# Stated amounts of filler at the priority of the work around them, in a streaming-trunk layer on one core

## The chip, the core and the metric

The kernel runs on one core of a Trainium2 chip. TensorE (PE in the rows; PEld for its weight loads) multiplies into PSUM; VectorE (DVE), ScalarE (ACT) and GpSimd (POOL) work on tiles in SBUF; SyncE (SP) issues the DMAs. Each engine takes its instructions in the order of its own queue and waits at semaphores. The metric is device time in microseconds for one execution, the median of several runs.

## The reference, cut to what matters

One layer over 1024 prompt frames and 32 sample frames (together T = 1056), width 1024, in float32:

```
xn = rmsnorm(h);  u_a, u_b, v_b, q, k, v, gates = split(xn @ w_in)      # 256,256,256,512,512,512,3*1024
y_a = S5 state-space(u_a) -> gelu -> GLU          # branch A
y_b = u_b * (lower-triangular W_s per 128-chunk applied to layernorm(v_b))     # branch B, "sgu"
y_c = stick-breaking attention(q, k, v), 8 heads of 64                # branch C
h = h + (sum_i sigmoid(gates_i) * (y_i @ w_branch_i)) @ w_out
h = h + (silu(xn2 @ w_gate) * (xn2 @ w_up)) @ w_down, xn2 = rmsnorm(h);   y = rmsnorm(h)
```

It also returns k, v, the end states of the state-space branch and the normalised v_b of the sample rows.

## The kernel before, in words

Every float32 matrix product is three fast products, high by high, low by high and high by low part (`mm3`, lines 144 to 146). A weight unit is 128x1024 elements: a DMA into raw, a rounded copy wh by ACT (line 117), the remainder wl by POOL (line 118), in a ring of four. Tokens stand in two halves, 512 and 544 wide; `CHUNKS` cuts them into 512, 272 and 272 columns. So one unit of 128 output features over all tokens is 72 products (24 per chunk), and over the first half alone 24 products of 512 columns.

The first phase (to about 719 us of the trace) runs, in program order: norm and transposes of x; `s5_setup` (small DVE work on the state-space parameters, with a few transposes and products); `v_dense` (values); the query and key tasks of head pairs 0 and 1; `sgu`; `ua_dense` and `s5_main` (state space); `attention`. Beside them stands a list of filler tasks: `qk_dense` for each of four head pairs (k and q, 72 products each) and `gate_ahead`, the gate products with sigmoid for 7 blocks of the first half and 4 of the second, three branches each; their results go to DRAM (sig_d, line 949) and are fetched in the second phase. `fill(us)` takes steps of filler off the list until their estimated PE time adds up to us; `finish` takes all of one task. In `sgu` there is no fill.

A list scheduler then makes each engine's queue: of the instructions that it holds for ready it takes the one with the lowest priority number, which counts up in program order. From the sgu stage on, `fill` adds `low[0]` = 4000 (`LATER`) to that number around its steps (lines 957 to 961), so filler comes after everything within the next 4000 that is ready. What is left of the list is done behind the attention, before the second phase (gates and branches, output projection, feed-forward), which this change leaves alone.

PSUM has tags of two buffers each: t (transposes), z (scores and state space), d (all dense products of the first phase), av (attention output, key transposes, the GLU).

Attention runs 32 units (head pair, block of 256 rows tp, head h2; the last pair with tp reversed). `stage_a`: two loads of q (line 768), score products into z (lines 781 to 785), a sigmoid on ACT (787), a reversed running product on DVE (789). `stage_b`: transposes of the weights (811), a split by ACT and DVE (819, 820), products with the values into av (828, 829). `load_head` (lines 736 to 752) brings a head's keys kst and its value differences vt; the single load at line 747 is one row. It is called when the first `stage_a` of the head runs, which is one unit ahead of its `stage_b`. The sample rows' attention stands after unit 30.

In `s5_main`, U is loaded from DRAM (line 624), V = products of U (631), a DVE chain of ten large operations makes the state (641 to 653), the end state is transposed (660), the output products follow (677 to 679), a gelu, a round trip through DRAM, a split on DVE (699) and the GLU.

## Time and profile before

| | us |
|---|---|
| runs shown | 1815.08, 1830.27, 1834.05; median 1830.27 |
| the profiled execution | 1818.52 |
| its span, first to last instruction | 1816.8 |
| PE busy | 1702.1 (94%) |
| DVE, ACT, POOL busy | 692.2, 521.7, 534.7 |
| mean granted TensorE clock | 0.973 |

Busy times are of all instructions of an engine; a busy PE isn't PE at its peak, since matmuls overlap. The granted clock is a share of 2.4 GHz. In a group row, "idle before" is idle time of the engine just before these instructions, with what ended it.

### The profile page before, as it was taken

The page shows a single profiled execution, that of the slowest core. Times are in us where ns is not written, and L with a number is a line of the kernel's source. Part 1 is how long each engine was busy: PE and PEld are TensorE (multiplying, and loading weights), DVE is VectorE, ACT ScalarE, POOL GpSimd, SP SyncE. Part 2 cuts the span into 40 slices and gives each one's busy share as a digit, 9 for nine tenths or more (in the row PEclk, how much of TensorE's full clock was granted, in tenths as well). Part 3 has the DMA queues.
Part 4 walks back from the last instruction along what each step waited for, and adds up shares of the span by engine and source line. Part 5 has one row for each costly group of instructions (what it writes and reads, how often), then busy time and mean ns, then how long its engine had stood idle before and what let it go on. Part 6 is the DMA issues. An engine that isn't in the chain of part 4 may idle for free.

```text
span 1816.8 us, 25700 instructions
## 1 busy us (share of the span) xinstructions
PE 1702.1 (94%) x10421; PEld 1502.1 (83%) x10421; DVE 692.2 (38%) x1387; ACT 521.7 (29%) x914; POOL 534.7 (29%) x333
## 2 busy tenths in 40 slices
PE   6889898978878999999999899999999999999997
PEld 6888787756656798889998899889889888888886
DVE  7954516228888100550266601230230321321315
ACT  5222232326656232222223322112111111111124
POOL 3211212320002242534443233233323333333334
PEclk9999999989999899999999999999999999999999
DMA  6544252555455453773362211111111111111102
GB/s 192 133 101 104 86 131 77 160 175 136 131 129 147 165 158 91 223 255 96 91 193 67 82 47 47 41 32 56 38 45 47 47 47 47 47 47 47 47 24 96
DMA packets 246487, 178.18 MB, mean 98 GB/s; under 512 B 60060, under 2 KB 222912, under 8 KB 246368
## 3 DMA queue, kind: packets, MB, share of 16 engines
q1 hardware_dynamic: 246368, 176.53, 33.4%
q8 instruction: 82, 1.34, 0.3%
q14 instruction: 37, 0.30, 0.1%
HBM read 136.69 MB, written 39.21 MB: 97 GB/s over the span
## 4 chain that ended last, share of the span: by engine, by line
PE 62%; DVE 7%; DMA 3%; SPq 3%; issue 2%; ACT 1%; POOL 1%; POOLq 0%; DVEq 0%; ACTq 0%
PE p L146 18%; PE p L145 18%; PE p L144 18%; DMA vt<-v_d 2%; PE p_d L146 2%; PE p_d L144 2%; PE p_d L145 2%; DVE om L789 2%; SPq L747 1%; PE p L1179 1%; DVE rs_m L169 1%; DVE wtl L820 1%; POOL wl L118 1%; DMA raw<-in_w_in_dram 0%; DVE xb L181 0%
## 5 line engine op out<-in xcount | busy, mean ns | idle before, releaser
L118 POOL TENSOR_TENSOR wl<-raw,wh 128x1024 fp32r<-128x1024 f32 x164 | 402.1, 2458 | 889.8 <-ACT wh L117 836.7
L145 PE MATMUL p<-x,wh 128*128 128x272 f32 (+1 forms) x1056 | 342.5, 324 | 0.0
L144 PE MATMUL p<-x,wh 128*128 128x272 f32 (+1 forms) x1056 | 341.5, 323 | 0.0
L146 PE MATMUL p<-x,wl 128*128 128x272 f32 (+1 forms) x1056 | 341.5, 323 | 0.0
L117 ACT ACTIVATE wh<-raw 128x1024 fp32r<-128x1024 f32 x164 | 172.7, 1059 | 482.0 <-PE p L146 185.0
L144 PE MATMUL p_d<-xnh,wh 128*128 128x272 f32 (+1 forms) x648 | 222.1, 343 | 9.0 <-DVE QS L313 4.4
L146 PE MATMUL p_d<-xnh,wl 128*128 128x272 f32 (+1 forms) x648 | 220.2, 340 | 1.3 <-POOL wl L118 1.3
L145 PE MATMUL p_d<-xnl,wh 128*128 128x272 f32 (+1 forms) x648 | 219.8, 339 | 0.0
L144 PEld LDWEIGHTS p<-x,wh 128*128 128x128 f32 x1056 | 198.9, 188 | 16.0
L145 PEld LDWEIGHTS p<-x,wh 128*128 128x128 f32 x1056 | 198.8, 188 | 15.9
L1135 DVE TENSOR_TENSOR sl<-p,sl 128x272 f32<-128x272 f32 (+1 forms) x66 | 34.6, 525 | 463.8 <-PE p L146 463.8
L146 PEld LDWEIGHTS p<-x,wl 128*128 128x128 f32 x1056 | 198.7, 188 | 15.3
L144 PEld LDWEIGHTS p_d<-xnh,wh 128*128 128x128 f32 x648 | 125.9, 194 | 21.0 <-DVE QS L313 4.8
L1138 POOL TENSOR_TENSOR act<-sl,act 128x512 fp32r<-128x512 f32 (+2 forms) x66 | 61.1, 925 | 279.0 <-ACT act L1136 279.0
L1189 DVE TENSOR_TENSOR h<-p,h 128x512 f32<-128x512 f32 x160 | 108.1, 687 | 79.3 <-PE p L146 79.3
L145 PE MATMUL p<-wl,act 128*128 128x512 f32 x352 | 137.1, 390 | 1.2 <-POOL wl L118 1.2
L146 PE MATMUL p<-wh,act 128*128 128x512 f32 x352 | 137.1, 389 | 0.0
L144 PE MATMUL p<-wh,act 128*128 128x512 f32 x352 | 136.9, 389 | 0.0
L146 PEld LDWEIGHTS p_d<-xnh,wl 128*128 128x128 f32 x648 | 125.4, 194 | 12.0 <-POOL wl L118 1.7
L145 PEld LDWEIGHTS p_d<-xnl,wh 128*128 128x128 f32 x648 | 125.8, 194 | 10.3 <-issue 0.5
L789 DVE TENSOR_TENSOR_SCAN om<-om 128x128 f32<-128x128 f32 (+3 forms) x64 | 91.1, 1435 | 3.0 <-ACT om L787 3.0
L1061 DVE TENSOR_TENSOR acc<-p,sgg 128x272 f32<-128x272 f32 (+1 forms) x24 | 12.4, 522 | 200.4 <-PE p L146 200.4
(383 smaller groups left out, 3071.4 us busy)
## 6 DMA issues: line engine op xcount, KB each, us to landing
raw<-in_w_in_dram SPq DMA_DIRECT2D x66, 512.0 KB
raw<-in_w_gate_up_dram SPq DMA_DIRECT2D x44, 512.0 KB
raw<-in_w_down_dram SPq DMA_DIRECT2D x22, 512.0 KB
q<-q_d SPq DMA_DIRECT2D x64, 128.0 KB
raw<-in_w_out_dram SPq DMA_DIRECT2D x16, 512.0 KB
sig_d<-sga SPq DMA_DIRECT2D x21, 256.0 KB
sgg<-sig_d SPq DMA_DIRECT2D x21, 256.0 KB
y<-y_d SPq DMA_DIRECT2D x16, 272.0 KB
```

The source lines that it names most:

```text
L117: s.activation(wh, raw, AF.Copy)
L118: g.tensor_sub(wl, raw, wh.bitcast(F32))
L144: pe.matmul(ps, ah, bh, start=start, stop=False)
L145: pe.matmul(ps, ah, bl, start=False, stop=False)
L146: pe.matmul(ps, al, bh, start=False, stop=stop)
L169: v.scalar_tensor_tensor(t, y, mh, y, op0=OP.mult, op1=OP.mult)
L747: sp.dma_start(tl[127:128, 8:12], v_d[hp][0:1, None, 64 * h2:64 * h2 + 64].to_broadcast([1, 4, 64]))
L789: v.tensor_tensor_scan(rev, rev, rev, 1.0, op0=OP.mult, op1=OP.bypass)
L820: v.tensor_sub(wl[:, lo:512], pt[:, lo:512], wh[:, lo:512].bitcast(F32))
L1135: v.tensor_mul(sl[:, 0:n], pu, sl[:, 0:n])
L1138: g.tensor_sub(act[:, e, T + TS + t0:T + TS + t0 + p], sl[:, 0:p], act[:, e, t0:t0 + p].bitcast(F32))
L1189: v.tensor_add(hr[:, cs], ps, hr[:, cs])
```

## The change

- `fill` no longer lowers the priority: filler stands at the priority of the place where it is called. The amounts change: `fill(1.5)` per block in sgu (new); in `s5_main` 10, 12, 12, then 24 (before 8, 18, 14), the 1.3 per GLU product kept; 8 before the first attention unit (new), 14 in the sample's attention (new); attention steps times 0.7 (before 1.0).
- Up to attention, dense products alternate between PSUM tags av and d (`ps_dense`), key transposes and the GLU use t.
- `next_unit` issues the load and split of the next filler unit when a filler unit starts.
- `s5_setup` is a generator in four parts, with `v_dense` and the two query/key tasks between them.
- Attention loads a head and its q two units ahead (`ahead`, `load_q`; q2 has three buffers), and finishes the head pair's query/key task there. ty is a half of yo.

```diff
-    LATER, SOONER = 4000, 1000
+    SOONER = 1000
+        early = [True]
+        turn_d = [0]
+        def ps_dense():
+            turn_d[0] += 1
+            return ps_tile("av" if early[0] and turn_d[0] % 2 else "d")
+        def ps_side():
+            return ps_tile("t" if early[0] else "d")
...
+        def next_unit(c0):
+            assert unit_order[unit_at[0]] == c0
+            unit_at[0] += 1
+            unit = unit_next.pop() if unit_next else fm_unit(win, c0)
+            if unit_at[0] < len(unit_order):
+                unit_next.append(fm_unit(win, unit_order[unit_at[0]]))
+            return unit
...
-                ps = ps_tile("d")[0:rows, 0:256]
+                ps = ps_dense()[0:rows, 0:256]
...
                 if b == 8:
                     sp.dma_start(sgu_v_s[0, 0], VN[0:32, 8])
+                fill(1.5)
...
-            fill(8)
+            fill(10)
...
             Z = W
+            fill(12)
             cmul(v, Q[:, 0], Q[:, 1], Z[:, 0], Z[:, 1], Er, Ei, X[:, 0], X[:, 1])
+            fill(12)
...
-            fill(18)
...
-            fill(14)
+            fill(24)
...
-                if (hp, h2) not in heads:
-                    heads[hp, h2] = load_head(hp, h2)
...
-            ratio = 1.0
+            ratio = 0.7
+            def ahead(i):
+                if i < len(units):
+                    hp, tp, h2 = units[i]
+                    if (hp, h2) not in heads:
+                        finish(qk_tasks[hp])
+                        heads[hp, h2] = load_head(hp, h2)
+                    load_q(hp, tp, h2)
+            for i in range(2):
+                ahead(i)
+            fill(8)
             ws = run_a(units[0])
             for i, u in enumerate(units):
+                ahead(i + 2)
...
         def fill(us):
             credit[0] += us
-            tc.cur_priority += low[0]
-            fill_(us)
-            tc.cur_priority -= low[0]
...
-                S = s5_setup(s5t, s5k)
+                S = {}
+                setup = s5_setup(s5t, s5k, S)
+                next(setup)
                 v_dense(pv)
+                next(setup)
                 finish(qk_tasks[0])
+                next(setup)
                 finish(qk_tasks[1])
-            low[0] = LATER
+                for _ in setup:
+                    pass
...
+        early[0] = False
```

What this does to the queues is shown at three places. First SP's queue around the state-space input, of before and then of the change: us_d is the input on its way through DRAM, U what is loaded from it, q_d and k_d stores of filler queries and keys, raw a weight load.

```order
133 L619 DMA us_d<-ua 128x1072
134 L113 DMA raw<-in_w_in_dram 128x8x128
135 L619 DMA us_d<-ua 128x1072
136 L113 DMA raw<-in_w_in_dram 128x8x128
137 L306 DMA k_d_69<-qe 64x2x272
138 L624 DMA U<-us_d 16x16x134 x8
139 L306 DMA k_d_69<-qe 64x2x272 x3
```

```order
140 L331 DMA q_d_65<-qe 64x2x272 x2
141 L653 DMA U<-us_d 16x16x134
142 L331 DMA k_d_70<-qe 64x2x512 x2
143 L331 DMA k_d_70<-qe 64x2x272 x2
144 L653 DMA U<-us_d 16x16x134
145 L331 DMA k_d_70<-qe 64x2x272 x2
146 L653 DMA U<-us_d 16x16x134
147 L331 DMA q_d_66<-qe 64x2x512 x2
148 L331 DMA q_d_66<-qe 64x2x272 x2
149 L653 DMA U<-us_d 16x16x134
150 L331 DMA q_d_66<-qe 64x2x272 x2
151 L653 DMA U<-us_d 16x16x134 x3
```

The eight loads of U stood together; now they are spread between the stores of filler queries and keys, the last three behind the last query store of head pair 3.

Second PE's queue in the attention of the last head pair: p_z scores, p_t transposes, p_av products with the values, p_d filler (gates).

```order
2534 L828 MATMUL p_av<-wd_3613,vt 128x256
2535 L811 MATMUL p_t<-ident,om 128x128 x4
2536 L781 MATMUL p_z<-kst,q_5481 128x512
2537 L782 MATMUL p_z<-kst,q_5481 128x512
2538 L829 MATMUL p_av<-wd_3614,vt 128x256
2539 L828 MATMUL p_av<-wd_3613,vt 128x256
2540 L829 MATMUL p_av<-wd_3614,vt 128x256
2541 L811 MATMUL p_t<-ident,om 128x128 x4
```

```order
2754 L845 MATMUL p_t<-ident,om 128x128 x4
2755 L144 MATMUL p_d<-xnh_141,wh 128x272
2756 L145 MATMUL p_d<-xnl_142,wh 128x272
2757 L146 MATMUL p_d<-xnh_141,wl 128x272
2758 L815 MATMUL p_z<-kst,q_5475 128x512
2759 L816 MATMUL p_z<-kst,q_5475 128x512
2760 L815 MATMUL p_z<-kst,q_5475 128x512
2761 L816 MATMUL p_z<-kst,q_5475 128x512
2762 L819 LDWEIGHTS identb
2763 L819 MATMUL p_z<-maskb,identb 128x128
2764 L144 MATMUL p_d<-xnh_141,wh 128x272
```

Three gate products now stand between nearly all steps of that pair; before, attention steps followed each other.

Third SP's queue where attention ends, with the tiles' numbers: y_d7_0 is the last attention output, sig_d0_4_2 the gate of the first half, block 4, branch 2, and y0_0 a load of the second phase.

```order
L949 DMA sig_d0_4_1_91<-sga_4989 128x512
L113 DMA raw_5580<-in_w_in_dram 128x8x128
L847 DMA y_d7_0_125<-yo_6331 64x2x256 x2
L949 DMA sig_d0_4_2_92<-sga_5112 128x512
L113 DMA raw_5701<-in_w_in_dram 128x8x128
```

```order
L997 DMA sig_d1_2_0_105<-sga_6598 128x272
L997 DMA sig_d1_2_1_106<-sga_6632 128x272
L881 DMA y_d7_0_125<-yo_6575 64x2x256 x2
L997 DMA sig_d1_2_1_106<-sga_6660 128x272
L1076 DMA y0_0_6928<-y_d0_0_111 128x512
```

Where before the first half's block 4 was being stored as attention ended, with blocks 5 and 6 and all four blocks of the second half (12 units) to come, it now is the second half's block 2.

## Rows read from the trace of the kernel before

**Rows 1.** The page, busy time, share of the span, instructions.

```profile
PE 1702.1 (94%) x10421; PEld 1502.1 (83%) x10421; DVE 692.2 (38%) x1387; ACT 521.7 (29%) x914; POOL 534.7 (29%) x333
```

**Rows 2.** Busy time by stage: PE, PEld, DVE, ACT, POOL, granted clock, DMA share, GB/s.

```profile
75.00:150.00 75.00, 64.34 (x392) 57.46 (x392) 44.70 (x89) 18.73 (x37) 13.06 (x7) 0.91 0.43 106
150.00:194.00 44.00, 37.64 (x255) 33.78 (x253) 24.52 (x97) 13.28 (x44) 6.93 (x4) 0.96 0.34 88
...
246.00:403.00 157.00, 138.68 (x776) 114.50 (x774) 55.99 (x69) 45.76 (x79) 37.23 (x18) 0.96 0.53 142
403.00:542.00 139.00, 114.63 (x681) 88.49 (x682) 116.15 (x134) 80.51 (x161) 3.50 (x1) 0.95 0.50 132
542.00:598.00 56.00, 44.59 (x281) 35.27 (x279) 45.26 (x55) 31.63 (x63) 14.55 (x20) 0.96 0.48 132
598.00:719.00 121.00, 120.51 (x773) 110.31 (x774) 3.83 (x11) 31.16 (x50) 38.31 (x16) 0.95 0.45 142
```

**Rows 3.** The same view: a stretch of 128x512 products, one of 128x272.

```profile
613.00:638.00 25.00, 25.00 (x109) 20.21 (x108) 0.24 (x1) 5.71 (x8) 7.22 (x3) 1.00 0.84 291
650.00:675.00 25.00, 25.00 (x201) 25.00 (x200) 0.00 (x0) 7.07 (x13) 10.34 (x5) 1.00 0.52 155
```

**Rows 4.** PE, 75 to 150: waits (total, times, longest), then instructions by time.

```profile
PE p_z L551 <- DVE big L42: 3.7, 1, 3.7
PE p_z L584 <- DVE CAr L42: 1.8, 1, 1.8
...
80.67 0.58 PE L144 MATMUL p_d<-wh,xnh 128*128 128x256 f32 x1 [5.21 <-DVE v L136]
81.05 0.41 PE L145 MATMUL p_d<-wl,xnh 128*128 128x256 f32 x1
81.26 0.41 PE L146 MATMUL p_d<-wh,xnl 128*128 128x256 f32 x1
```

**Rows 5.** PE's waits, 150 to 194.

```profile
PE p_d L144 <- ACT vb L351: 3.6, 2, 2.5
```

**Rows 6.** State space: PE's waits, 246 to 403, then DVE by time.

```profile
PE p_d L144 <- DVE QS L313: 4.4, 1, 4.4
PE p_z L660 <- DVE Q L668: 1.1, 1, 1.1
...
266.32 1.27 DVE L641 TENSOR_TENSOR Q<-Er,V 128x1064 f32<-128x1064 f32 x1 [3.29 <-ACT V L633]
...
291.60 0.16 DVE L658 COPY fin<-W 128x8 f32<-128x8 f32 x1
...
309.59 2.39 DVE L684 TENSOR_TENSOR V<-Q 128x2144 f32<-128x2144 f32 x1 [17.01 <-ACT Q L680]
...
339.41 2.39 DVE L699 TENSOR_TENSOR yl<-U,yh 128x2144 fp32r<-128x2144 f32 x1 [16.51 <-ACT yh L698]
```

**Rows 7.** The chain that ended last, 366 to 406: start, us, what.

```profile
378.32 9.11 DMA vt<-v_d
...
391.91 7.35 SPq L747
```

**Rows 8.** DVE, 403 to 598: its longest wait, then its two costliest groups.

```profile
DVE va L750 <- DMA vt<-v_d: 11.9, 5, 3.0
...
L789 DVE TENSOR_TENSOR_SCAN om<-om 128x384 f32<-128x384 f32 (+7 forms) x62 | 90.0, 1463 | 2.6 <-ACT om L787 2.6
L820 DVE TENSOR_TENSOR wtl<-p_t,wth 128x512 fp32r<-128x512 f32 x48 | 31.7, 672 | 7.9 <-ACT wth L819 7.9
```

**Rows 9.** One line's instructions, the one-row load: duration ns min/median/max, first, last.

```profile
L747 SPq DMA_DIRECT2D vt<-v_d x8: 631/7098/7351, 378.3 to 544.0; - x8
```

**Rows 10.** Busy time as in rows 2, the tail's beginning.

```profile
598.00:613.00 15.00, 14.51 (x59) 11.16 (x60) 3.58 (x11) 3.27 (x5) 2.34 (x1) 0.57 0.13 30
```

**Rows 11.** The chain as in rows 7, 719 to 728: a weight unit's way.

```profile
719.07 4.11 DMA raw<-in_w_in_dram
...
726.80 0.79 PE p L146
```

More of the change, by code (lines that the diff above doesn't have):

```diff
@@ L262, in v_dense @@
                 tc.cur_priority += SOONER
+        unit_order = [(768 + 512 * which + 128 * hp) for hp in range(4) for which in (1, 0)]
+        unit_order += [2304 + 1024 * br + 128 * m for h in range(2) for m in range(AHEAD[h]) for br in range(3)]
+        unit_at = [0]
+        unit_next = []
+        def next_unit(c0):
[5 more added lines that the diff above has]
+            return unit
         def qk_dense(wk, hp):
@@ L288, in qk_dense @@
             for which in (1, 0):
-                unit = fm_unit(win, 768 + 512 * which + 128 * hp)
+                unit = next_unit(768 + 512 * which + 128 * hp)
                 dst = (q_d, k_d)[which][hp]
                 for h, o, n, t0 in CHUNKS:
-                    ps = ps_tile("d")[:, 0:n]
+                    ps = ps_dense()[:, 0:n]
                     for i, c in enumerate(fm_steps(ps, unit, xn[h], o, n)):
@@ L348, in sgu @@
                 else:
-                    ps = ps_tile("d")[0:rows, 0:256]
+                    ps = ps_dense()[0:rows, 0:256]
                     tm_dense(ps, xn[h], off, rows, us)
@@ L391, in sgu, with s5_setup @@
                     sp.dma_start(d[:, :, o:o + w], yo[:, :, 0:w].bitcast(F32))
-        def s5_setup(pl, keep):
+        def s5_setup(pl, keep, out):
             rows = pl.tile([128, 128], F32, name="rows")
@@ L769, in stage_a @@
                                  q_d[hp][h2].rearrange("l d t -> d l t")[:, :, 256 * tp:256 * tp + 256])
+                qs[hp, tp, h2] = q2
+            def stage_a(hp, tp, h2):
+                kst = heads[hp, h2][0]
+                q2 = qs.pop((hp, tp, h2))
                 ws = []
@@ L857, in run_a @@
                 return ws
+            def ahead(i):
[8 more added lines that the diff above has]
+            fill(8)
             ws = run_a(units[0])
             for i, u in enumerate(units):
+                ahead(i + 2)
                 nxt, done = None, True
                 if i + 1 < len(units):
-                    if (units[i + 1][0], 0) not in heads:
-                        finish(qk_tasks[units[i + 1][0]])
                     nxt = stage_a(*units[i + 1])
@@ L900, in sample_attention @@
             po = ps_tile("av")
+            fill(2)
             for gr in range(2):
@@ L905, in sample_attention @@
                     pe.matmul(z[:, 0:160], QS[r, hp, :], KS[r, hp, :], start=(e == 0), stop=(e == 3))
+                fill(4)
                 sg = wk.tile([128, 160], F32, name="sgs", bufs=2)
@@ L925, in sample_attention @@
                 v.tensor_copy(wt[0:32, 128:256], pt[0:32, 128:256])
+                fill(2)
                 for e in range(4):
@@ L940, in gate_ahead @@
             for br in range(3):
[L941 removed]
+                unit = next_unit(2304 + 1024 * br + 128 * m)
                 for h, o, n, t0 in CHUNKS:
```

34 lines of the change are left out of this document (17 added, 17 removed).

## The prediction

> **What bounds the kernel now.** I read the page's head first: TensorE (PE) is busy 94% of 1816.8 us [rows 1], so the end can only come sooner if PE waits less or works faster. The table by stage says where it doesn't work [rows 2]. From 598 to 719 us PE is busy 120.5 of 121 us and every other engine nearly idle: pure filler (gate products) that found no room earlier. From 403 to 598 (attention) VectorE (DVE) is busy 116.2 of 139 and 45.3 of 56 us while the weight loads (PEld) fill 63% of the time. That is the pattern of the case: a stretch that DVE bounds, followed by one that only PE needs. After 719 us nothing changes in order or amount, and I cost it at zero.
>
> Prices of filler [rows 3]: a stretch of 128x512 products alone holds 109 in 25 us, 0.229 us each; one of 128x272 alone 201, 0.124 us each; one of 128x256 by its columns 0.117.
>
> **How much work moves.** The counts are of the order. Behind the last attention product stood 165 products of 512 columns and 576 of 272; now 249 of 272 (the last pair of rows in the change's section shows the border). So 165 x 0.229 + 327 x 0.124 = 78.3 us leave the tail. They go to three places: the sgu stage gets 18 of 512 and 48 of 272 (+10.1 us); the state-space stage loses those and gets 193 of 512 (+44.2 - 10.1 = +34.1); attention gets 327 of 272 and loses 28 of 512 (+34.1). What matters is how much of each is hidden.
>
> **Set-up, 75 to 150 us.** PE waits 5.2, 3.7 and 1.8 us, each time for DVE [rows 4]. The first is a full PSUM ring: tag d has two buffers, one held by a 64-row block whose add stands in DVE's queue behind the set-up chain. The change alternates d and av, four buffers, so two more blocks fit (24 x 0.117 = 2.8, and 24 x 0.229 + 48 x 0.124 = 11.5 us of work) before that buffer is wanted: gone. The other two are PE reaching set-up transposes ahead of DVE; they now stand after the whole first query/key task, some 20 us of work later, while DVE's chain is as long as before. After the first wait products of 256 columns start 0.21 us apart [rows 4] and not 0.117: half clock (1.2 of 2.4 GHz). The stage's granted clock of 0.91 [rows 2] makes 0.18 x 75 = 13.5 us at half clock, at most 6.7 us lost. Bounds -5.2 (first wait only) to -17.4 (all); I take -14.
>
> **sgu, 150 to 194 us.** 208 products of 256 columns (24.3 us) and 21 of 512 (4.8) stand in 44 us; PE waits for the evacuation of vb [rows 5]. With `fill(1.5)` behind each block and four buffers PE has 29.1 + 10.1 = 39.2 us of work there, and some small transposes: 43 us, -1. If nothing is absorbed +10.1; at best -3.
>
> **State space, 246 to 403 us.** PE is busy 138.7 of 157 us [rows 2], so the added 34.1 us are mostly on the path: no gain is lost by that, since they leave the tail at the same price. New wait: the eight loads of U now stand on SP between the stores of q2, k3 and q3, the last three behind q3 (first pair of order rows). PE has 41 us of filler meanwhile (54 products of q2, 72 each of k3 and q3, 48 of two gates), so nothing waits, but V's products come late and only 61 products of 512 (14 us) are left to cover DVE's chain from V to the state output, which took from 266.32 to 291.76 [rows 6]. Without the four query/key operations between, about 24 us: a wait of 10 us. The waits of 4.4 and 1.1 us there now [rows 6] end, since gates are evacuated by ScalarE alone; small waits for U's landing may add 1 to 2. Behind the output stand 179 products (41 us) against the gelu round trip through DRAM, 309.59 to 339.41 until its data are split again [rows 6]: covered. Attention's first loads remain as they are: vt 9.1 us, then 7.4 us of SP for the second head [rows 7]; they are queued behind the same stores as now, so PE's wait there stays. Sum 34.1 + 10 - 5.5 - 2.6 = +36, the last a part of the slow clock (0.96 [rows 2]). Bounds +24 (no new wait) to +42.
>
> **Attention.** DVE's idle time of the first three head pairs is first of all the wait for vt, 11.9 us in 5 waits over 403 to 598 [rows 8]; the one-row load of vt keeps SP 7.1 us in the median [rows 9]. Heads and q now are loaded two units ahead (a unit is 195/32 = 6 us), so both are hidden: -8 for 403 to 542, where the scans and splits (90.0 + 31.7 us over all heads [rows 8]) then bound. There 9 of the 34.1 us land, in PE's free 24 us. The other 25 land in the last head pair, three products between all steps (second pair of order rows), 542 to 598. By the busy row PE has 56 - 44.6 = 11.4 us free there: it overruns by 14 us. By weight loads, 35.3 us at the tail's rate of 110.3 in 121 [rows 2] are 38.7 us of work, 17.3 free: overrun 8. I take +10. Attention as a whole: +2, with -8 (all absorbed) and +34 (none) as ends.
>
> The Trainium skill (Perfetto Trace Analysis, Identifying the Most-Contended Engine) says that matmul busy time misleads and that headroom is read from weight loads; by it the sum would be 2 us less, by the busy row 4 us more. Which is right no row of this kernel shows; the changed kernel's last head pair will.
>
> **Tail, 598 to 719 us.** 249 x 0.124 = 30.9, with start and end 33 us: -88. That is more than the 78.3, because 598 to 613 ran at a clock of 0.57 [rows 10] with the sample's small products in it; these now stand in attention under filler. Bounds -80 to -90.
>
> Sum: -14 - 1 + 36 - 8 + 10 - 88 = -65. The profiled execution took 1818.5 us, so 1753.5. The median of the runs shown is 1830.3 (1815.1 to 1834.1), 11.8 above it; which of the two an execution falls to isn't in the profile, so I add a part, 4.5: **1758 us**. What no term names (ratio 0.7, ty in half of yo, k_out and the gated products in tag t, the unit prefetch) costs nothing: no instruction is added, and the ring of four weights keeps two free under a unit of 11.5 us while a load with its split takes about 8 (719.07, the load's issue, to 726.80, the first product of wl [rows 11]). Without that cover each unit would pay what is over.
>
> **Rivals.** *In order, nothing absorbed.* PE runs its queue in order, so a gate product ahead of a transpose delays it, the split behind it and the next product. For: the last head pair has filler between all steps, and its DVE idles only 10.7 of 56 us. Against: in the first pairs PE waits between steps anyway. Then attention pays +34 less 8 rather than +2: 1758 + 24 to 32, about 1786. The Trainium skill (TensorE: Matmul & The Clock Gate, Part 3, The mechanism) states that matmuls keep strict order; what it costs here was worked out from rows.
>
> *Everything fits.* The V wait is covered and the last pair absorbs its 25 us: 1758 - 10 - 10 - 3 = 1735. For: the weight-load reading.
>
> *Slower: SP's queue blocks.* Loading two units ahead, vt's third buffer is free only when the head two before it is done; SP waits for it in order, and behind it stand q2, gate stores and weights. If each of the six later heads paid a 7.1 us issue plus a landing of 9.1 [rows 7, 9] in the open: 6 x 16.2 = 97, 1855 us. It becomes slower than before from (1830 - 1758)/6 = 12 us a head. Against: all of that is in the queue today, one unit later, and DVE's open waits for it are 11.9 us in all.
>
> *The change doesn't do what it says:* the order shows the filler moved; what could fail is only the hiding, the first rival.
>
> **Chances.** Forecast 0.60 (1745 to 1775), nothing absorbed 0.20, everything fits 0.14, SP 0.04, else 0.02. Range 1728 to 1794: from below "everything fits" with set-up's better end to the first rival with the state-space stage's worse one. About 1% is what a measurement of this kernel can tell from no change: below 1812 us is faster, 0.94; within 0.03; slower 0.03.
>
> **What would show it.** PE without the 5.2 us wait for v; a wait of about 10 us before the fin transpose, the forecast's weakest term; no DVE wait for vt beyond the first two heads; last attention product near 613 us, gate stage near 650 instead of 719; the last head pair 64 to 68 us long. The forecast is wrong if attention as a whole takes over 205 us, or if the state-space stage gains more than 42 us.

## The result, and the profile after

The changed kernel takes 1807.62 us in the median (1801.91 to 1817.14, 12 runs), the one before 1830.12 (1815.08 to 1836.12): a ratio of 0.9892 with an interval of 0.9863 to 0.9922. The forecast was 1758, its range 1728 to 1794. The direction was right; of the 65 us that the sum took off one profiled execution, the changed kernel's own (1807.88, span 1806.1) shows 10.7. One kernel's runs lie up to 21 us apart, and the profiled execution of before (1818.52) lies 11.6 us below its median, so the traces can show only about half of the 22.5 us between the medians; what follows is compared by stage, in the traces, with the medians beside it.

The page's head of the changed kernel, to be held against [rows 1]:

```profile
PE 1696.1 (94%) x10421; PEld 1505.0 (83%) x10421; DVE 700.2 (39%) x1387; ACT 519.7 (29%) x914; POOL 535.7 (30%) x333
```

The same work in the same shares. Where the stages lie now is told by the first and last start of a few lines of the changed kernel: the transposes of the spatial weights (L358), the last spatial product (L403), the scores (L815), the last products with the values (L863), and by the first product of the second phase in its timeline:

```profile
L358 PE MATMUL p_t<-ident,WT x4: 272/273/329, 144.0 to 144.4; 128*128 128x128 f32 x4
...
L403 PE MATMUL p_z<-WT,VN x8: 218/228/238, 210.9 to 224.9; 32*64 32x32 f32 x8
...
L815 PE MATMUL p_z<-kst,q x96: 276/396/775, 429.9 to 654.6; 128*128 128x384 f32 x40, 128*128 128x512 f32 x32, 128*128 128x256 f32 x24
...
L863 PE MATMUL p_av<-wd,vt x64: 274/283/581, 435.1 to 682.3; 128*128 128x256 f32 x64
...
716.89 0.50 PE L144 MATMUL p<-xnh,wh 128*128 128x512 f32 x1 [2.98 <-ACT wh L117]
```

The same in the trace of before:

```profile
L333 PE MATMUL p_t<-ident,WT x4: 272/272/273, 149.0 to 149.3; 128*128 128x128 f32 x4
...
L377 PE MATMUL p_z<-WT,VN x8: 218/228/238, 206.3 to 220.3; 32*64 32x32 f32 x8
...
L781 PE MATMUL p_z<-kst,q x96: 278/418/775, 389.2 to 584.4; 128*128 128x384 f32 x40, 128*128 128x512 f32 x32, 128*128 128x256 f32 x24
...
L829 PE MATMUL p_av<-wd,vt x64: 277/283/562, 394.5 to 609.3; 128*128 128x256 f32 x64
...
724.37 0.80 PE L144 MATMUL p<-xnh,wh 128*128 128x512 f32 x1 [3.21 <-ACT wh L117]
```

That gives the stages (us); the sum's tail began at 598, so attention and tail are compared together:

| | before | after | change | forecast |
|---|---|---|---|---|
| start to spatial weights (set-up) | 149.0 | 144.0 | -5.0 | -14 |
| sgu | 71.3 | 80.9 | +9.6 | -1 |
| state space, to the first score | 168.9 | 205.0 | +36.1 | +36 |
| attention, to the last product with the values | 220.1 | 252.4 | +32.3 | |
| tail | 115.1 | 34.6 | -80.5 | |
| attention and tail | 335.2 | 287.0 | -48.2 | -86 |
| second phase | 1092.4 | 1089.2 | -3.2 | 0 |

The filler left the tail as counted and was paid again where it went: sgu, state space and attention are together 78.0 us longer, for the 78.3 us of filler that the prediction counted into them. Busy time by stage of the changed kernel (PE, PEld, DVE, ACT, POOL, granted clock, DMA share, GB/s), to be held against [rows 2]:

```profile
78.00:144.00 66.00, 57.49 (x360) 51.63 (x358) 41.98 (x80) 19.52 (x40) 15.08 (x7) 0.92 0.53 139
144.00:225.00 81.00, 71.61 (x520) 66.08 (x519) 35.24 (x127) 22.15 (x61) 11.03 (x6) 0.94 0.27 72
225.00:430.00 205.00, 193.40 (x1032) 160.06 (x1031) 62.21 (x73) 61.41 (x97) 59.63 (x27) 0.97 0.48 138
430.00:682.00 252.00, 213.20 (x1334) 182.08 (x1335) 171.41 (x201) 124.00 (x248) 32.91 (x27) 0.91 0.47 128
```

PE's free time is still there, 38.8 us of it in attention (42.1 before, between the same marks). Its waits in the first two stages, to be held against [rows 4, 5], first 70 to 144 us, then 144 to 226:

```profile
PE p_t L304 <- ACT kt L306: 8.5, 1, 8.5
```

```profile
PE p_d L144 <- ACT vb L376: 7.0, 1, 7.0
PE p_d L146 <- POOL wl L118: 1.2, 1, 1.2
PE p_av L144 <- ACT k L328: 1.2, 1, 1.2
```

The waits for v, big and CAr are gone, as the prediction said, and one for the key transposes has come in their place; the wait for vb is longer than before.

### The profile page after: what moved, and what is told of

The parts are those of the page before. It is cut to its first block, busy times and chain, and to the rows that moved or that the text cites. A ratio compares the mean times of both kernels' runs of the same rounds, so it can differ in the third digit from the quotient of the medians.

```text
span 1806.1 us, 25695 instructions
## 1 busy us (share of the span) xinstructions
PE 1696.1 (94%) x10421; PEld 1505.0 (83%) x10421; DVE 700.2 (39%) x1387; ACT 519.7 (29%) x914; POOL 535.7 (30%) x333
## 4 chain that ended last, share of the span: by engine, by line
PE 73%; DVE 12%; DMA 7%; issue 3%; ACT 2%; SPq 2%; POOL 2%; POOLq 0%; DVEq 0%; ACTq 0%
PE p L146 18%; PE p L145 18%; PE p L144 18%; PE p_d L144 3%; PE p_d L146 3%; DMA vt<-v_d 3%; PE p_d L145 3%; DVE om L823 2%; DMA raw<-in_w_in_dram 2%; PE p_av L144 1%; PE p_av L146 1%; POOL wl L118 1%; PE p_av L145 1%; DVE rs_m L169 1%; PE p L1226 1%
## 5 line engine op out<-in xcount | busy, mean ns | idle before, releaser
L146 PEld LDWEIGHTS p<-x,wl 128*128 128x128 f32 x1056 | 198.5, 188 | 15.2
L144 PE MATMUL p_d<-xnh,wh 128*128 128x272 f32 (+1 forms) x464 | 162.6, 351 | 12.3 <-ACT vb L376 7.0
L146 PE MATMUL p_d<-xnh,wl 128*128 128x272 f32 (+1 forms) x464 | 158.6, 342 | 6.7 <-POOL wl L118 6.7
L145 PE MATMUL p_d<-xnl,wh 128*128 128x272 f32 (+1 forms) x464 | 157.2, 339 | 0.0
L144 PEld LDWEIGHTS p_d<-xnh,wh 128*128 128x128 f32 x464 | 92.5, 199 | 20.0 <-ACT vb L376 7.2
L146 PEld LDWEIGHTS p_d<-xnh,wl 128*128 128x128 f32 x464 | 91.9, 198 | 15.4 <-POOL wl L118 8.4
L145 PEld LDWEIGHTS p_d<-xnl,wh 128*128 128x128 f32 x464 | 92.0, 198 | 6.5
L1183 ACT ACTIVATE act<-sl 128x272 fp32r<-128x272 f32 (+1 forms) x66 | 32.5, 492 | 190.8 <-DVE sl L1182 190.8
```

The source lines that it names most:

```text
L144: pe.matmul(ps, ah, bh, start=start, stop=False)
L145: pe.matmul(ps, ah, bl, start=False, stop=False)
L146: pe.matmul(ps, al, bh, start=False, stop=stop)
L1183: s.activation(act[:, e, t0:t0 + n], sl[:, 0:n], AF.Copy)
```

## The experiments

All are edits of the changed kernel. Their times, with the ratio to the kernel before:

| | median (lowest to highest, runs) | ratio, interval |
|---|---|---|
| changed kernel | 1807.62 (1801.91 to 1817.14, 12) | 0.9892, 0.9863 to 0.9922 |
| e1_attn_none | 1819.67 (1814.64 to 1829.81, 10) | 0.9989, 0.9956 to 1.0021 |
| e3_heads_one | 1802.23 (1801.20 to 1804.18, 4) | 0.9876, 0.9834 to 0.9918 |
| e7_vt4 | 1797.28 (1795.58 to 1798.88, 4) | 0.9823, 0.9795 to 0.9851 |
| e8_row_memset | 1802.00 (1800.15 to 1807.49, 4) | 0.9854, 0.9823 to 0.9886 |
| e11_z_only | 1803.89 (1801.21 to 1806.94, 4) | 0.9857, 0.9821 to 0.9893 |
| e14_sig_queue | 1794.75 (1792.17 to 1796.18, 4) | 0.9850, 0.9807 to 0.9893 |
| e16_sq_first | 1804.54 (1802.92 to 1809.62, 4) | 0.9866, 0.9823 to 0.9909 |
| e4_sgu_none | 1814.63 (1801.03 to 1820.02, 10) | 0.9926, 0.9888 to 0.9963 |
| e5_d_queue | 1796.53 (1795.51 to 1797.82, 4) | 0.9820, 0.9792 to 0.9848 |
| e6_setup_one | 1815.49 (1807.44 to 1824.18, 10) | 0.9941, 0.9907 to 0.9974 |
| e13_k_pool | 1803.91 (1802.87 to 1820.49, 7) | 0.9916, 0.9878 to 0.9954 |
| e10_u_queue | 1814.17 (1809.39 to 1818.54, 10) | 0.9948, 0.9918 to 0.9977 |
| e15_d_among | 1817.21 (1810.13 to 1818.77, 9) | 0.9935, 0.9905 to 0.9965 |
| c1_combo | 1795.47 (1788.22 to 1798.28, 4) | 0.9849, 0.9802 to 0.9897 |
| c5_dq_sq | 1794.55 (1791.94 to 1795.84, 4) | 0.9806, 0.9757 to 0.9855 |
| c6_dq_sq_vt4 | 1793.62 (1791.51 to 1795.43, 4) | 0.9801, 0.9761 to 0.9842 |

Attention in kernels that hold the changed kernel's attention order took 252.4 (changed), 246.6 (e5) and 249.1 us (e13): less than 6 us of difference in one profile's attention is not read.

### Does attention hide filler?

**e1_attn_none**: no filler stated in attention.

```diff
-            ratio = 0.7
+            ratio = 0.0
-            fill(2)
             for gr in range(2):
...
-                fill(4)
...
-                fill(2)
```

> The changed kernel, but attention states no filler: its steps' amounts times 0 and nothing in the sample's attention. By the order 27 products of 512 and 270 of 272 less stand between the first score and the last product with the values, and they stand in the tail instead (61.2 us of filler in attention become 25.6, the tail's 30.9 us become 66.5). Theory A, filler in attention costs its own time since PE takes its queue in order: attention from first score to last product with the values falls from 252 us to 217 to 222, the tail rises from 35 to 70, and the total stays within 6 us of the changed kernel's 1807.6. Theory B, attention is longer for another reason, the loads two units ahead: attention stays above 240 us and the total rises by 20 to 36 us. The prediction's own step (32 us more work, 24 of it hidden) would make the total 24 us longer.

Attention took 223.1 us, 29.3 less for 35.6 us less of filler, and the tail 71.6, 37.0 more: 6 to 8 us had been hidden, not 24. That is theory A in the main. Its total missed: the median lies 12.1 us above the changed kernel's, where theory A allowed 6. In the profile attention and tail are together 7.7 us longer and the state-space stage 11.4, with its output products at half clock (28.8 us instead of 17.1, below).

**e16_sq_first** asks the same of the last two pairs and the sample alone, on top of e14 (below):

```diff
+                ratio = 0.7 if i < 16 else 0.0
                 for c in stage_b(*u, ws):
                     fill(ratio * c)
```

with the sample's amounts out as in e1.

> As e14 (gates' stores from GpSimd's queue), but with no filler stated in attention's last two head pairs and in the sample. By the order hp2, hp3 and the sample then hold 16.7 us instead of 39.5, the tail 53.7 instead of 30.9. Theory A, the last two pairs hide nothing and the sample about half of its 12 us: from the third pair's first score to the last product with the values 17 to 20 us shorter than in e14, the total 1795 to 1802 (e14 1794.8). Theory B, the forecast's step (more than half of that filler is hidden): the total 1807 or more.

From the third pair's first score to the last product with the values it took 119.1 us, e14 135.3: 16.2 less, for 22.8 us of filler, so 6.6 had been hidden. The sample holds most of that: it took 17.6 instead of 24.2 us, 6.6 less for 12.0 less of filler. The pairs gave back 9.6 for 10.8: they hide next to nothing. The total lies halfway, 2.5 us above theory A's end and 2.5 below theory B's; by the stages, 6.6 of 22.8 us hidden is less than the half that theory B asks for.

Filler against length, from the third pair's first score to the sample's first score product (filler counted in the order, at the prices of [rows 3]):

| | filler, us | length, us |
|---|---|---|
| before | 12.8 | 105.6 |
| e16 | 14.2 | 101.5 |
| e14 | 25.0 | 111.1 |
| changed | 36.6 | 133.0 |

In the windows view, this stretch of before, of the changed kernel, of e14 and of e16, one line each:

```profile
485.00:591.00 106.00, 87.73 (x531) 69.51 (x531) 90.19 (x105) 62.38 (x123) 10.82 (x4) 0.95 0.51 140
```

```profile
525.00:658.00 133.00, 113.34 (x739) 99.05 (x739) 96.08 (x107) 70.96 (x137) 24.24 (x9) 0.92 0.49 134
```

```profile
532.00:643.00 111.00, 96.14 (x680) 83.98 (x679) 92.31 (x106) 66.43 (x132) 23.94 (x15) 0.97 0.52 141
```

```profile
535.00:637.00 102.00, 87.85 (x596) 75.14 (x595) 89.58 (x104) 62.32 (x126) 16.70 (x10) 0.97 0.52 141
```

PE is idle 18.3 us of this stretch before, 19.7 after, 14.9 and 14.2 in e14 and e16. 208 more products went in and PE's idle time did not shrink. Most of it stands in front of products of weights and values (p_av) that wait for a split on VectorE. PE's two longest waits of the stretch before, then of the changed kernel (total, times, longest):

```profile
PE p_av L829 <- DVE wtl L820: 10.1, 13, 1.6
PE p_z L781 <- DMA q<-q_d: 5.0, 2, 3.2
```

```profile
PE p_av L863 <- DVE wtl L854: 12.8, 11, 4.0
PE p_av L863 <- DVE wd L854: 4.1, 2, 3.7
```

What is queued behind such a product can't step into its gap, and what is queued ahead of the work that feeds it delays that work. This is read from the queues; no run changes the order rule itself. PEld filled 66% before and 74% after. The Trainium skill (Perfetto Trace Analysis, Identifying the Most-Contended Engine) reads headroom from that share; here there was room by both readings, busy and weight loads, and neither was usable. Why the last 11.6 us of filler (e14 to the changed kernel) cost 22 stays open. The clock, 0.97 in e14 and 0.92 in the changed kernel, doesn't explain it, since e5, with the same filler there, ran at 0.97 and took 131.2 us. The buffers of vt may have a part in it: e7 (below), with a fourth, holds 39.3 us of filler there in 125.4 us, 14.3 more than e14 for 14.3 more.

**e11_z_only** states the same amounts beside score steps only.

```diff
+                owed = 0.0
                 for c in stage_b(*u, ws):
-                    fill(ratio * c)
+                    owed += ratio * c
...
-                            fill(ratio * c)
+                            fill(ratio * c + owed)
+                            owed = 0.0
```

> The changed kernel with the same amounts of filler in attention, but stated only beside the score steps, none between a transpose step and the product step behind it. By the order the stages hold the same amounts within 0.5 us. Theory A, what costs is filler that stands in PE's strict order between a transpose, its split and its product: attention falls by 6 to 15 us from 252, the total as much. Theory B, PE itself is full where the filler lies (the last head pair and the sample), so the place within a step is of no matter: attention and total stay within 4 us.

248.6 us of attention, which is what e13 took with the places unchanged: theory B, though not by its reason, a full PE, since PE is idle 18.5 us of the same stretch there. The place of the filler within a step is no cause; what matters is that it lies in those stages.

**e14_sig_queue**: the gates' stores go out from GpSimd's queue.

```diff
-                    sp.dma_start(sig_d[half][m][br][:, o:o + n], sg)
+                    g.dma_start(sig_d[half][m][br][:, o:o + n], sg)
```

> The changed kernel with the gates' stores issued from GpSimd's queue instead of SP's. By the order filler then spreads more evenly over attention (first pair 11.0 us instead of 4.1, the last two 25.0 instead of 36.6), the tail holding the same 30.9. Theory A, filler is never absorbed by attention's gaps, wherever it stands: attention changes by the amount that it holds (57.2 instead of 61.2 us, so 3 to 6 us shorter), the total stays within 4 us. Theory B, it is absorbed where PE waits for the first heads' loads, and not in the last pairs: attention falls by 10 us or more, the total by 6 or more.

Theory B on the total, 12.9 us below the changed kernel (all four runs lie below its lowest). The first pair took 47.5 us with 11.0 us of filler, and 46.9 with 4.1 in the changed kernel: there PE waits for the heads' loads, and filler is free. It could not get there, because a gate's result holds one of two buffers (sga) until its store has left, and the stores stood behind the head loads on SP. Attention as a whole fell to 228.9 us; the state-space stage gave back 10 (215.0).

### Two units ahead

**e3_heads_one**

```diff
-            for i in range(2):
-                ahead(i)
+            ahead(0)
...
-                ahead(i + 2)
+                ahead(i + 1)
```

> The changed kernel, with heads and q loaded one unit ahead as before instead of two. Theory A, the second unit gains nothing, since the load of a later head waits for a free buffer of vt and VectorE's subtraction for vt stands at the same place of its queue either way: VectorE's waits for vt over the last six heads stay 15 us within 4, and the total within 6 us of 1807.6. Theory B, the loads ahead are what lengthens attention: attention falls by 10 us or more, the waits for vt to 12 or less. The prediction's step (8 us gained by the second unit) would make it 8 us longer, the waits for vt 20 or more.

VectorE's waits for vt over the last six heads: 12.2 us, attention 247.9, the total 1802.23, all within theory A. The second unit gains nothing. VectorE's waits in the changed kernel, 446 to 650 us, to be held against [rows 8]:

```profile
DVE wtl L854 <- ACT wth L853: 19.9, 15, 4.1
DVE va L780 <- DMA vt<-v_d: 15.2, 5, 4.5
```

**e7_vt4** gives vt a fourth buffer.

```diff
-                vt = at.tile([128, 12, 2, 64], F32R, name="vt", bufs=3)
-                vb = vt[:, :, 1, :].bitcast(F32)
-                for tl, r0 in ((va, 0), (vb, 1)):
+                vt = at.tile([128, 12, 2, 64], F32R, name="vt", bufs=4)
+                vc, vb = [vt[:, :, e, :].bitcast(F32) for e in range(2)]
+                for tl, r0 in ((vc, 0), (vb, 1)):
...
-                v.tensor_sub(va, va, vb)
+                v.tensor_sub(va, vc, vb)
```

with one pair of wd, and two q2 loaded one unit ahead.

> The changed kernel with a fourth buffer for vt; both loads of the values go straight into vt, so that they no longer wait for va. To make room one pair of wd instead of two and two buffers of q2, loaded one unit ahead. Theory A, loading two units ahead gains nothing because the odd heads' loads wait for a buffer of vt: VectorE's waits for vt over the last six heads fall from 15.2 us to 5 or less, attention from 252 to 238 to 246 us, the total falls by 6 to 12 us. Theory B, the waits for vt are covered by the filler anyway: attention stays within 4 us of 252.

The same view, 450 to 650 us:

```profile
DVE va L780 <- DMA vt<-v_d: 5.7, 2, 4.3
...
DVE va L780 <- DMA y_d<-yo: 1.7, 1, 1.7
```

7.4 us instead of 15.2 (theory A said 5 or less), and a total of 1797.28: waiting for buffers held the loads back, theory A. The edit does two things, the fourth buffer of vt and the load straight into vt past va. SP's waits at these loads in the changed kernel, 446 to 650 us:

```profile
SPq L774 <- PE p_av L863: 7.5, 2, 4.2
SPq L774 <- PE p_t L845: 3.2, 1, 3.2
SPq L774 <- DVE vt L782: 2.7, 2, 2.0
```

The first two stand ahead of loads of vt, the last ahead of loads of va, so most of the waiting is for vt's buffers; e7 has none there. In the profile attention is 231.6 us, but 4 us of filler moved ahead of it and the first score comes 11 us later after the GLU. From the last GLU product to the last product with the values it takes 267.8 us, against 277.6 in the changed kernel and 272.5 in e5, which has the same filler there: a gain of 5 to 10 us.

**e8_row_memset** takes away the one-row load whose 7 us stood in [rows 9].

```diff
                     if r0:
+                        g.memset(tl[96:128, 8:12], 0.0)
                         sp.dma_start(tl[0:127, 8:12], src[0:127, 1::2])
-                        sp.dma_start(tl[127:128, 8:12], v_d[hp][0:1, None, 64 * h2:64 * h2 + 64].to_broadcast([1, 4, 64]))
```

> The changed kernel, where the single row of vt is set to zero by GpSimd ahead of the load of the other 127 rows, instead of by a transfer of its own (the eight issues of 6.7 to 7.4 us on SP). Theory A, the 7 us belong to that transfer: they leave SP, the landing after it too, each head's vt is there about 7 us sooner, VectorE's waits for vt fall from 41 us in all to 25 or less, and attention and the total fall by 8 to 16 us. Theory B, the 7 us are the time in which the earlier pieces of the head's load (3072 pieces of 256 bytes) drain, and SP's next issue inherits them: the next q load takes the 7 us, the waits for vt and the total stay within 4 us.

SP's timeline of e8 at the first head (start, us; here L777 is the load of 127 rows, L797 that of q):

```profile
414.59 1.32 SPq L774 DMA_DIRECT2D vt<-v_d  x1
418.25 0.25 SPq L777 DMA_DIRECT2D vt<-v_d  x1
418.59 7.28 SPq L797 DMA_DIRECT2D q<-q_d  x2
```

Over all eight heads, the load of L777 and that of q (L797), of the changed kernel (where L777 is the one row) and then of e8 (ns min/median/max, first, last):

```profile
L777 SPq DMA_DIRECT2D vt<-v_d x8: 6662/7040/7443, 419.1 to 589.0; - x8
...
L797 SPq DMA_DIRECT2D q<-q_d x64: 573/599/992, 426.2 to 640.5; - x64
```

```profile
L777 SPq DMA_DIRECT2D vt<-v_d x8: 249/395/436, 418.3 to 585.9; - x8
...
L797 SPq DMA_DIRECT2D q<-q_d x64: 573/598/7406, 418.6 to 635.8; - x64
```

The 7 us have moved to the next load in line: theory B. VectorE's waits for vt from 400 to 680 us stay at 41.0 us (41.3 in the changed kernel); the median falls by 5.6 us, between theory B's 4 and theory A's 8. The prediction read the 7 us as the price of that one row; they fall to whichever load stands behind the head's pieces in the queue. That they are the time in which those pieces drain, as theory B has it, fits but isn't shown by itself.

### Set-up and sgu

**e4_sgu_none** leaves the filler out of sgu (`fill(1.5)` removed).

> The changed kernel without the 1.5 us of filler behind each block of sgu; by the order 10.1 us of filler leave sgu and stand later. Theory A, a filler key store on SP's queue stands ahead of the last nine copies of the state-space matrix D, whose source gives its memory to sgu's first vb: with the store gone PE's wait for vb falls from 7.0 to under 4 us, sgu from 80.9 to 64 to 68 us, and the total falls by 3 to 6 us. Theory B, the filler in sgu costs only its own time: sgu falls by 10 us to 71, the total stays within 2 us.

sgu fell by 9.7 us to 71.2 for 10.1 us of filler: next to nothing had been hidden (theory B). The wait for vb stayed, 6.9 us, so the filler stated in sgu is not its cause. The total did not stay within theory B's 2 us: the median is 7.0 us above the changed kernel's. The state-space output products of this profile ran at half clock too (0.51, 29 us).

**e5_d_queue**

```diff
-                    sp.dma_start(D[16 * j:16 * j + 16, 8 * g2:8 * g2 + 8, 16 * j:128], KK[16 * g2:16 * g2 + 16, :, 0:128 - 16 * j])
+                    g.dma_start(D[16 * j:16 * j + 16, 8 * g2:8 * g2 + 8, 16 * j:128], KK[16 * g2:16 * g2 + 16, :, 0:128 - 16 * j])
```

> The changed kernel with the sixteen copies into the state-space matrix D issued from GpSimd's queue instead of SP's; PE's order is the same. Theory A, sgu's first vb waits for these copies because SP has them behind a filler key store: PE's wait for vb falls from 7.0 us to 3 or less, sgu from 80.9 to 73 to 77 us, the half-clock stretch at 165 to 175 shortens, and the total falls by 4 to 8 us. Theory B, the vb wait has another last cause (the products of the filler or ScalarE's order): the wait and sgu stay within 2 us.

In the changed kernel SP issues nine of these copies behind a key store, and ScalarE takes the first vb only after them (SP's, then ScalarE's timeline):

```profile
145.01 4.54 SPq L631 DMA_DIRECT2D D<-KK  x7
159.99 1.28 SPq L331 DMA_DIRECT2D k_d<-qe  x2
161.64 5.84 SPq L631 DMA_DIRECT2D D<-KK  x9
```

```profile
169.29 0.38 ACT L376 ACTIVATE vb<-p_d 128x256 f32<-128x256 f32 x1 [5.98 <-DMA out_dram<-kt]
```

KK, from which the matrix D is copied, lies in the set-up's pool of buffers. That pool is closed ahead of sgu's, so sgu's buffers take its memory and wait for the copies that read it. (The row names a key store that SP issues right behind the copies, and e5 brings that store forward too, from 167.59 to 162.30 us. That the wait is for the copies is read from the program.) With the copies on GpSimd's queue PE's wait for vb is 1.2 us, sgu 72.7 (8.2 less) and the median 1796.53: theory A, and the largest single gain found beside e14's. That is 11.1 us, more than the 4 to 8 expected.

**e6_setup_one** puts the set-up back in one part ahead of the values.

```diff
-                next(setup)
+                for _ in setup:
+                    pass
                 v_dense(pv)
-                next(setup)
                 finish(qk_tasks[0])
-                next(setup)
                 finish(qk_tasks[1])
-                for _ in setup:
-                    pass
```

> The changed kernel with the state-space set-up in one part ahead of the values, as before; PSUM tags, amounts and all else as changed. Theory A, the split only exchanges waits: the wait of 8.5 us for the key transposes' evacuation at 97 to 107 us goes, the waits for big and CAr (5.5 us before) come back, the first spatial-weight transpose stands at 140 to 146 us (changed 144), and the total stays within 6 us. Theory B, the split is what gained the 5 us of set-up: that transpose stands at 149 or later, and the total rises by 5 us or more.

PE waits 12.2 us for big and 1.8 for CAr, where the changed kernel waits 8.5 for kt. The total is 8 us above the changed kernel's by medians and 5.5 by the lowest runs, as theory B has it; to the last spatial product, with the same filler, the profile shows 3.2 us (228.1 against 224.9). The split is worth 3 to 8 us. (The transposes named come at 162.7 us, since 9 us of filler moved ahead of them; they are no mark here.)

**e13_k_pool** takes the low part of the first pair's keys off VectorE.

```diff
-                    v.tensor_sub(qe[:, 1, 0:n], full, qe[:, 0, 0:n].bitcast(F32))
+                    (g if which and hp == 0 else v).tensor_sub(qe[:, 1, 0:n], full, qe[:, 0, 0:n].bitcast(F32))
```

> The changed kernel, where the low part of the first head pair's keys is made by GpSimd instead of VectorE (three operations). Theory A, PE's wait of 8.5 us for the key transposes' evacuation is VectorE's set-up chain, ahead of the keys' low part, which holds both qe buffers: the wait falls to 3 us or less, the half-clock stretch at 100 to 110 goes, the first spatial-weight transpose comes 6 to 10 us earlier than 144, and the total falls by 5 to 10 us. Theory B, PE reaches a set-up transpose instead and waits there as long (as the kernel before did, 5.5 us): the total falls by 3 us at most.

PE's only wait in 70 to 144 us is now another:

```profile
PE p_z L579 <- ACT BT L580: 9.7, 1, 9.7
```

Theory B. In the changed kernel the keys' low part stands among the set-up chain on VectorE, and ScalarE's evacuation waits for the store behind it (its timeline):

```profile
104.43 0.40 ACT L325 ACTIVATE qe<-p_av 128x272 fp32r<-128x272 f32 x1 [12.32 <-DMA k_d<-qe]
```

In e13 it is the queries' high part that stands so (ScalarE's timeline of e13):

```profile
111.79 0.40 ACT L325 ACTIVATE qe<-p_d 128x272 fp32r<-128x272 f32 x1 [9.34 <-DMA q_d<-qe]
```

Freed of the keys, PE runs on to the set-up's transposes at 102.7 us and waits there for their evacuation (BT), which ScalarE does only behind this instruction. The query store that this one waits for needs the queries' low part, and VectorE makes that at 106.8 us, behind the chain, which e13 left as it was. So the edit moved the wait from the keys to the queries. The chain on VectorE stays the bound of this stage by either way; the total is 3.7 us lower by medians.

### The state space

**e10_u_queue** issues U's loads from GpSimd's queue (`g.dma_start(U[...` for `sp.dma_start(U[...`).

> The changed kernel with the eight loads of U issued from GpSimd's queue, so that they no longer stand between SP's stores of filler queries and keys. By the order 42 products of 512 move from ahead of V to behind it. Theory A, V's products come late because U's loads stand behind those stores, and VectorE's chain then lies bare: V's products start at 283 us or earlier instead of 291, the stretch from the last V product to the fin transpose stays 29 us long but holds 18.5 us of filler instead of 14, and the total falls by 4 to 8 us. Theory B, what fills that stretch is set by when the gates' weights land, not by when it starts: it grows as V comes earlier, and the total stays within 3 us.

V's products started at 280.9 us, the stretch to the fin transpose took 27.2, and the total rose to 1814.17: neither theory. The start of the fin transpose is 12.6 us earlier than in the changed kernel; what ate that are the output products behind it. In the windows view, those of the changed kernel, then of e10:

```profile
325.00:342.00 17.00, 17.00 (x95) 12.88 (x93) 0.28 (x1) 4.78 (x8) 4.77 (x3) 0.98 0.22 64
```

```profile
313.00:343.00 30.00, 30.00 (x95) 22.53 (x96) 0.24 (x1) 4.18 (x7) 4.68 (x2) 0.50 0.13 36
```

The same products (95 of them in either row) at 1.2 instead of 2.4 GHz, 13 us.

**e15_d_among** puts filler ahead of and among them (`fill(12)` of the 24 moved ahead, the products 150 places later).

> The changed kernel with the state-space output products 150 places later in the order and 12 of the 24 us of filler stated ahead of them: by the order 22 products of filler stand before them and single ones among them. Theory A, these products alone keep the half clock once they begin at it, which is what spreads a kernel's runs: their stretch shows a granted clock of 1.00 at every look, no run lies more than 6 us above the fastest, and the median is 1800 to 1804 (the lower end of the changed kernel's 1802 to 1817). Theory B, the spread comes from elsewhere: runs still reach 10 us above the fastest. Either way up to 5 us may be lost, since less filler is left for the gelu's way through DRAM.

The stretch showed a clock of 0.94 (1.00 but for its first 5 us), yet the median is 1817.21 and the runs reach 9 us above the fastest: theory A, which had 1800 to 1804 and 6 us, fails. With its filler the stretch takes 31.8 us, and the first GLU product comes at 395.9 us instead of 384.2. Whether the half clock there is what spreads one kernel's runs stays open; the profiles of e1, e4 and e10 show it, those of before and of the changed kernel don't.

### Put together

**c1_combo** is e5 with e7, **c5_dq_sq** e5 with e14, **c6_dq_sq_vt4** all three; the edits are those above.

> The changed kernel with the copies into D from GpSimd's queue and with four buffers of vt (the two edits that gained alone). Each alone came to 1797, some 8 us below the changed kernel's usual 1804. If the two waits are independent places of one path, the total is 1786 to 1791; if one gain hides behind the other, 1794 to 1798.

> The changed kernel with the copies into D and the gates' stores both from GpSimd's queue (e5 and e14 together; alone 1796.5 and 1794.8 against about 1804). Independent places: 1785 to 1789. If GpSimd's queue, which holds both and the weights' low parts, makes one wait for the other: 1793 or more.

> As c5 with four buffers of vt as in e7. e5 and e7 together came to 1795.5, hardly below either alone. If e7's and e14's gains are the same one (filler and loads of the first heads): within 3 us of c5. If they add: 5 us or more below c5.

1795.47, 1794.55 and 1793.62: each pair comes out near its better half, as the second case of c1's and c5's expectations has it, and c6 lies within 3 us of c5. In c5 sgu keeps its 8 us (72.7), and the state-space stage grows to 218.3 us from e14's 215.0 and e5's 206.0. Why they don't add is shown in part: in e14 and c5 PE waits 1.7 us for GpSimd's and 1.7 us for ScalarE's part of a weight unit between the output products and the GLU, where e5 and the changed kernel don't wait, and from 280 to 440 us GpSimd's queue in e14 stands 45.0 us for gates whose stores it is to issue. c6 beats both kernels: 0.9801 of before (0.9761 to 0.9842), some 14 us below the changed one; e14 and e5 alone are as good within what these runs tell.

## Why the prediction was wrong

**Prices and counts** held: the tail fell by 80.5 us against 78.3 counted, and nothing after it moved by more than 3.2 us. **The weight of the forecast lay on what is hidden, and there it failed**, at the places below. In attention's last pairs PE's own order is the reason: free time in front of a waiting product is closed to filler behind it. At the others it is a buffer, or the order of another engine's queue.

**Attention, the last pair.** The step that failed is "PE has 56 - 44.6 = 11.4 us free there", with an overrun of 10 taken for 25 us of filler. The last two pairs together got 23.8 us of filler and took 27.4 longer, with PE's idle time as long as before. Only the sample hid some, 6.4 of 12.0, and part of that is the clock. The sample of before, then of the changed kernel:

```profile
590.70:609.30 18.60, 15.25 (x73) 11.17 (x73) 4.22 (x13) 3.27 (x8) 6.07 (x17) 0.68 0.07 17
```

```profile
658.10:682.30 24.20, 24.20 (x176) 22.71 (x176) 4.79 (x13) 5.37 (x12) 8.57 (x19) 0.93 0.33 97
```

The first rival described this, at about 1786, with 0.20. It priced attention at +34 less 8; measured are +32.3, so its 34 was near and the 8 didn't come.

**Attention, the first pairs.** "so both are hidden: -8", of heads and q two units ahead, gained nothing (e3): the loads waited for buffers (e7), of which vt has three. The forecast named that buffer, in the SP rival, as a danger from going two units ahead, and didn't see that for the same reason going ahead can't help. "There 9 of the 34.1 us land, in PE's free 24 us" failed too: the third pair got 5.7 us more than before and the first two 1.6 less, since their gate buffers were held (e14). The reading of the one-row load as 7 us of its own was wrong (e8). SP's queue did block, as the SP rival feared, but at other places: gate stores behind the heads' loads (e14) and, in sgu, copies behind a key store (e5).

**sgu.** -1 came out as +9.6. The wait for vb was taken for a matter of PSUM buffers; it belongs to the copies of KK, a queue that the prediction did not walk (e5). With these out of the way sgu takes 72.7 us with the same filler, 1.4 more than before.

**Set-up.** -14 came out as -5.0. That the transposes "now stand after the whole first query/key task" was right of PE's order and wrong of VectorE's: the chain stayed first there, so the keys' low part, and with it PE, waited for it instead; with the keys moved, the queries' low part did (e13). The prediction did not ask what is late next.

**State space.** +36 came out as +36.1, and that is in part luck. The 34.1 us of filler were on the path, as said; the wait of 10 us before the fin transpose did not come. The stretch from the last V product to it takes 29.3 us instead of 26.3 with 14.0 us of filler instead of 17.7. VectorE's chain was done at 323.0 us, PE came to the transpose at 325.2, because it had waited for the gates' weights (290 to 326 us) and run at half clock behind that:

```profile
PE p_d L146 <- POOL wl L118: 4.0, 2, 2.0
PE p_d L144 <- ACT wh L117: 3.9, 2, 2.6
```

**The range** went from the better outer rival to the worse, each with one more term at its end (by its own words that makes 1732 to 1792, not quite the 1728 to 1794 stated). The bad ends of the sum were -5.2, +10.1, +42, and for attention and tail +34 with -80: together +1. Set-up, sgu, and attention with the tail all went to or near theirs; the terms of sgu and attention hang on one assumption, that filler is hidden. And the 4.5 us for the median were not needed: the profiled execution of the changed kernel lies at its median.

**The signs** that it named: the wait for v is gone; the wait before fin did not come; VectorE's waits for vt did not end; the last product with the values came at 682.3 instead of 613, the gate stage at 716.9 instead of 650, and the last head pair, from its first score to the sample's first, took 69.6 us instead of 64 to 68. The sign "if attention as a whole takes over 205 us" came: that was 10 more than the prediction's 195 for before, and by the marks used here attention went from 220.1 to 252.4.

## What to carry to other kernels

Free time of an in-order engine is no room: look which instruction stands in front of each gap, and count as hidden only what can be queued ahead of that one without delaying the work that feeds it (filler was free in e14's first pair, where PE waits for loads, and paid in the last two, where it waits for splits of its own transposes). A load issued earlier gains nothing while its buffer is the one that is waited for; count the buffers before crediting the distance. And where several terms rest on one assumption, their bad ends belong in the range together.

## What was not expected of the hardware

A stretch of 133-column output products, the same in each kernel, ran at a granted clock of 0.98 to 1.00 in 17 us or at 0.50 in 30, and stayed at the lower level through its whole length in e10. What PE did before it there (windows of e10, columns as above):

```profile
300.00:305.00 5.00, 4.59 (x20) 3.38 (x18) 4.94 (x4) 0.74 (x1) 0.16 (x1) 1.00 0.52 157
305.00:310.00 5.00, 0.00 (x0) 0.00 (x0) 4.96 (x3) 0.80 (x2) 3.08 (x1) 0.66 0.02 4
310.00:315.00 5.00, 2.44 (x8) 1.85 (x9) 2.68 (x8) 1.06 (x1) 1.10 (x1) 0.50 0.54 159
```

An idle stretch, then the products, and PE counts as fully busy at half speed for 30 us. In the changed kernel PE also had idle time and the lower level ahead of the products, which begin at 325.4, and they ran at the upper (0.98 from 325 to 342 us, above):

```profile
315.00:320.00 5.00, 1.99 (x8) 0.97 (x6) 4.93 (x4) 1.54 (x2) 2.38 (x1) 0.88 0.02 7
320.00:325.00 5.00, 4.66 (x11) 3.61 (x12) 3.03 (x7) 0.58 (x1) 0.28 (x1) 0.50 0.50 157
```

What decides between the two stays open. The long issue of a small transfer (7 us) was not that transfer's: taken away, it appeared at the next one in line (up to 7.4 us, e8).
